# One change to a hybrid decoder layer: the 256-token blocks in plain float32 instead of rounded pairs

## The chip, the cores and the metric

The kernel is one launch on one core of one Trainium2 chip. The metric is the device time of that launch in microseconds. The core has TensorE (PE in the profile, with its weight loads as PEld), VectorE (DVE), ScalarE (ACT), GpSimd (POOL) and SyncE (SP), each with its own queue of instructions that it runs in order, and 16 DMA engines that all the queues share.

## The reference

One decoder layer on 1024 tokens of width 1024, all in float32. The input is normalised and projected; three branches read the projection (a state-space mixer with a short convolution, a gated mixer over positions, and cross-attention to 256 memory tokens), each goes through its own block of `w_branch`, is weighed by a sigmoid gate, and the sum goes through `w_out` and is added to x. Then a mixture of 16384 single-neuron experts is added: 8 heads, each with two sets of 128 keys, the best 16 of each set, the best 16 of their 256 sums. Shortened:

```
proj = rms_norm(x) @ w_in ; z, xbc, dt, u, v, q, gates = split(proj)
merged = sum_n sigmoid(gates_n) * (branch_n @ w_branch_n)      # ssd, gmlp, memory
x = x + merged @ w_out ; xt = rms_norm(x)
sc = (xt @ w_peer_q) . peer_keys ; top 16 per half ; top 16 of the sums -> eid, gate
x = x + sum_k gate_k * gelu(peer_u[eid_k] . xt) * peer_v[eid_k]
return rms_norm(x)
```

## The kernel before

**Tokens.** `BLOCKS` (line 24) are 256, 256 and 512 tokens. A block goes through `mixer` (line 316): 12 convolution tiles (`conv_tile`), the chunk steps of the state-space branch (`chunk_a`, `chunk_b`), z and v, the three branches, the output projection; then `routing` (line 661) chooses its experts. The routing of one block is written beside the convolutions and gates of the next (`beside`, `spill`), and it shares one buffer (`shared`) with the next block's second chunk step. Keys and values of the memory (`mem_norm`, `mem_kv`) are made first.

**Rounded pairs.** Every large product is taken in pairs. A weight tile of 128 x 1024 float32 is loaded by `unit` (line 167) into `raw`, cast by ScalarE to the rounded type float32r (`whi`, line 160), and its rest `wlo` is the difference, taken by GpSimd or, by a share `lo_dve`, by VectorE (line 161). Activations are split in the same way, on ScalarE and VectorE (lines 225, 247, 288, 553, 610, 628). `mm3` (lines 187 to 189) is then three matmuls: hi x hi, hi x lo, lo x hi. `feat` runs 8 such triples on one weight tile with features as output rows (256 or 512 columns, by the block's tokens); `tok` runs 4 weight tiles over all of a block's 128-token tiles with 512 columns. Small products (scores against the keys, attention, line 608, line 579) are plain float32 matmuls already. There are three `raw` buffers and every fourth unit of the mixer uses a fourth one, three `whi` and three `wlo`.

**Experts.** The first 512 tokens (the two blocks of 256) fetch their chosen rows: `gathered` (line 783) issues, for each of 4 tiles of 128 tokens, 128 gathers of u rows and 128 of v rows on GpSimd's queue, 1024 in all; VectorE multiplies each (lines 803 and 810). They are written last in the program. The last 512 tokens run densely over all 16384 experts (`gate_matrix`, `dense_act`, `dense`).

**What sets the order.** A planner places instructions by their position in the program unless `tc.cur_priority` is set, and lets an engine run what is ready. Each `unit` leaves a mark: its priority, its ACT cast (`first`), its subtraction (`second`, or the last one of GpSimd if VectorE took it), and a rate. `pace` (line 1012) picks a mark for a gather: for the first 37 slots (74 gathers) a mark of the second block's units or of the routing beside them, by the rates 0.25 and 0.36; then none up to slot 270; from there a mark of the dense stage. Where there is a mark, the gather takes its priority and `tc.issue_after(m0[2].ins)` (line 792) queues it behind that subtraction on GpSimd.

Of the kernel before, what the change touches and what calls it, by code (L numbers as in the profile page):

```python
# [8 lines left out]
F32 = mybir.dt.float32  # L9
# [49 lines left out]
def layer_kernel(ctx, tc, a, out_d):  # L59
# [104 lines left out]
    lo_dve, share = [0], [0.0]  # L164
    in_mix = [True]

    def unit(src, n=D, k=KD):
        prio = tc.cur_priority
        if in_mix[0] and len(marks) % 4 == 3:
            raw = tmp.tile([P, D], F32, tag="raw4", name="raw", bufs=1)  # L170
        else:
            raw = wts.tile([P, D], F32, tag="raw", name="raw")
        dst = raw[:, :n]
        if len(src.shape) == 3:
            dst = dst.rearrange("p (k c) -> p k c", k=src.shape[1])
        nc.sync.dma_start(dst, src)
        hi = wts.tile([P, D], F32R, tag="whi", name="whi")
        lo = wts.tile([P, D], F32R, tag="wlo", name="wlo")
        share[0] += lo_dve[0]
        on_dve = share[0] >= 1  # L180
        share[0] -= on_dve
        first, second = split(hi[:, :n], lo[:, :n], raw[:, :n], nc.vector if on_dve else nc.gpsimd)
        marks.append((prio, first, marks[-1][2] if on_dve and marks else second, rate[0]))
        return (hi[:, :n].rearrange("p (k c) -> p k c", k=k), lo[:, :n].rearrange("p (k c) -> p k c", k=k))
# [4 lines left out]
        nc.tensor.matmul(ps, lhsT=l_lo, rhs=r_hi, start=False, stop=stop)  # L189

    def feat(src, act, ps=None):
        hi, lo = unit(src)
        if ps is None:
            ps = mm_ps()[:, :act[0].shape[-1]]
        for k in range(KD):
            mm3(ps, hi[:, k, :], lo[:, k, :], act[0][:, k, :], act[1][:, k, :], k == 0, k == KD - 1)
        return ps

    def tok(src, act):
        nt = act[0].shape[-1] // P  # L200
        pss = [mm_ps() for _ in range(nt)]
        for kk in range(4):
            hi, lo = unit(src[kk], k=2)
            for t in range(nt):
                for j in range(2):
                    k = kk * 2 + j
                    s = slice(t * P, (t + 1) * P)
                    mm3(pss[t], act[0][:, k, s], act[1][:, k, s], hi[:, j, :], lo[:, j, :],
                        k == 0, k == KD - 1)
        return pss  # L210

    def act_tiles(n=T):
        if n <= T // 2:
            t = a16(F32R)
            return tuple(t[:, j * KD * n:(j + 1) * KD * n].rearrange("p (k t) -> p k t", k=KD) for j in range(2))
        return (a16(F32R).rearrange("p (k t) -> p k t", k=KD), a16(F32R).rearrange("p (k t) -> p k t", k=KD))

    def transposed(dst, src, t):
        ts = slice(t * P, (t + 1) * P)
        for k4 in range(2):  # L220
            ps = tp_ps()
            for j in range(4):
                k = k4 * 4 + j
                nc.tensor.transpose(ps[:, j * P:(j + 1) * P], src[:, k * P:(k + 1) * P], ident)
            split(dst[0][:, k4 * 4:k4 * 4 + 4, ts], dst[1][:, k4 * 4:k4 * 4 + 4, ts],
                  ps.rearrange("p (j t) -> p j t", j=4))


    def mem_norm():
        m_tok = b16().rearrange("p (t d) -> p t d", t=4)  # L230
        nc.sync.dma_start(m_tok[:, 0:2, :], a["mem"].rearrange("(t p) d -> p t d", p=P))
        ss = sml.tile([P, 2], F32, tag="ssm", name="ss")
        for t in range(2):
            sumsq(col(ss, t), m_tok[:, t, :], m_tok[:, 2 + t, :])
        r = rstd_of(ss, 2)
        for t in range(2):
            nc.vector.tensor_scalar(m_tok[:, t, :], m_tok[:, t, :], col(r, t), None, op0=ALU.mult)
        mT = a16(F32R)
        hi = mT[:, 0:2048].rearrange("p (k m) -> p k m", k=KD)
        lo = mT[:, 2048:4096].rearrange("p (k m) -> p k m", k=KD)  # L240
        for k in range(KD):
            ps = tp_ps()
            for t in range(2):
                nc.tensor.transpose(ps[:, t * P:(t + 1) * P], m_tok[:, t, k * P:(k + 1) * P], ident)
            g = col(pk, PK_LN_MEM + k)
            nc.scalar.activation(hi[:, k, :], ps[:, 0:256], AF.Copy, scale=g)
            nc.vector.scalar_tensor_tensor(lo[:, k, :], ps[:, 0:256], g, hi[:, k, :].bitcast(F32),
                                           op0=ALU.mult, op1=ALU.subtract)
        return hi, lo

    def mem_kv(mT):
        for f in range(8):
# [26 lines left out]
    def x_turn(x_sb, gains):  # L279
        TT = x_sb.shape[1]  # L280
        hT = act_tiles(TT * P)
        for k in range(KD):
            ps = tp_ps()
            for t in range(TT):
                nc.tensor.transpose(ps[:, t * P:(t + 1) * P], x_sb[:, t, k * P:(k + 1) * P], ident)
            g = col(pk, gains + k)
            nc.scalar.activation(hT[0][:, k, :], ps[:, :TT * P], AF.Copy, scale=g)
            nc.vector.scalar_tensor_tensor(hT[1][:, k, :], ps[:, :TT * P], g, hT[0][:, k, :].bitcast(F32),
                                           op0=ALU.mult, op1=ALU.subtract)
        return hT  # L290

    def conv_tile(f, hT, dst, turned):
        T = hT[0].shape[-1]
        ps = feat(a["win_a"][FA_XBC + f], hT)
        cw = PK_CONVW + f * 4
        ac = t2()[:, :T]
        nc.scalar.activation(ac, ps, AF.Identity, bias=col(pk, PK_CONVB + f), scale=col(pk, cw + 3))
        for j in range(3):
            s = 3 - j
            nc.vector.scalar_tensor_tensor(ac[:, s:T], ps[:, 0:T - s], col(pk, cw + j), ac[:, s:T],  # L300
                                           op0=ALU.mult, op1=ALU.add)
            nc.vector.scalar_tensor_tensor(ac[:, 0:s], hist[:, f, j:3], col(pk, cw + j), ac[:, 0:s],
                                           op0=ALU.mult, op1=ALU.add)
        nc.scalar.copy(hist[:, f, :], ps[:, T - 3:T])  # L304
        src = ac if dst is None else dst
        nc.scalar.activation(src, ac, AF.Silu)
        if turned is not None:
            tp = tp_ps()
            for c in range(T // P):
                nc.tensor.transpose(tp[:, c * P:(c + 1) * P], src[:, c * P:(c + 1) * P], ident)  # L310
            nc.scalar.copy(turned, tp[:, :T].rearrange("p (c d) -> p c d", c=T // P))
# [4 lines left out]
    def mixer(b, hT, lmt=None):  # L316
# [20 lines left out]
            nsm[0] += 1  # L337
            return bc[:, o:o + NS].rearrange("p (c h) -> p c h", c=TT)

        hi, lo = unit(a["w_dt"], n=128)  # L340
        fps = mm_ps()[:, :T]
        for k in range(KD):
            mm3(fps[0:16, :], hi[:, k, :], lo[:, k, :], hT[0][:, k, :], hT[1][:, k, :], k == 0, k == KD - 1)
        dtT = tT()
        nc.scalar.copy(dtT[0:16, :], fps[0:16, :])
        conv_tile(4, hT, None, xy[:, :, 4 * P:5 * P])
# [191 lines left out]
        for g in range(8):  # L538
# [11 lines left out]
                                           col(pk, PK_GMLP + g), bs[:, None, :].to_broadcast([P, TT, P]),  # L550
                                           op0=ALU.mult, op1=ALU.add)
            nc.gpsimd.tensor_tensor(m1, m1, ug, op=ALU.mult)
            split(yT[0][:, g, :], yT[1][:, g, :], m1)
        branch(1, yT)


# [47 lines left out]
        def values(h, pTs):  # L604
            for f in range(2):
                op = mm_ps()[:, :T]
                for j in range(2):
                    nc.tensor.matmul(op, lhsT=vm[:, j, h * 256 + f * P:h * 256 + (f + 1) * P], rhs=pTs[j],
                                     start=(j == 0), stop=(j == 1))
                split(yT[0][:, 2 * h + f, :], yT[1][:, 2 * h + f, :], op)  # L610

        prs = attend(0, query(0))
        for h in range(1, H_XA):
# [11 lines left out]

        mT = act_tiles(T)
        for k in range(KD):
            split(mT[0][:, k, :], mT[1][:, k, :], merged[:, k, :])
        ss2 = sml.tile([P, 2, TT], F32, tag="ss2", name="ss2")
        for j in range(2):  # L630
            pss = tok(a["out_b"][j], mT)
# [27 lines left out]


    def routing(xnT, rt, gt=None, eid=None, beside=lambda: None):
        T = xnT[0].shape[-1]
        TT = T // P
        NK = 16 * TT
        U = 16 * NK
# [117 lines left out]
    def gathered(tt, eid, gt, pace):  # L783
        rs = slice(tt * P, (tt + 1) * P)

        def rows_of(table, k, half):
# [2 lines left out]
            if m0:  # L789
                tc.cur_priority = m0[0]  # L790
            g = gat.tile([P, D], F32, tag=f"g4{k % NG}", name="g4", bufs=1)
            with (tc.issue_after(m0[2].ins) if m0 else nullcontext()):
                nc.gpsimd.indirect_dma_start(out=g, out_offset=None, in_=a[table],  # L793
                                             in_offset=bass.IndirectOffsetOnAxis(ap=eid[:, k:k + 1], axis=0))
            if m0:
# [5 lines left out]
        for k in range(SLOTS):  # L801
            g, m1 = rows_of("u", k, 0)
            nc.vector.scalar_tensor_tensor(g, g, 1.0, xn, op0=ALU.mult, op1=ALU.mult, accum_out=col(w, k))  # L803
        with (tc.issue_after(m1[1].ins) if m1 else nullcontext()):
            nc.scalar.activation(w, w, AF.Gelu_apprx_tanh)
        nc.vector.tensor_tensor(w, w, gt, op=ALU.mult)
        acc = held(x2_d[rs, :])
# [134 lines left out]
    for b in range(1, len(BLOCKS)):  # L942
# [12 lines left out]
        def spill(count):  # L955
            for _ in range(count):
                n, f = early.pop(0)
                T = hT[0].shape[-1]
                sgt = t2()[:, :T]
                sigmoid_gate(sgt, hT, n, f)  # L960
                nc.sync.dma_start(gate_d[b][n * KD + f], sgt)
# [9 lines left out]
        lo_dve[0] = 0 if b == 1 else LO_MIXER  # L971
        rate[0] = RATE_MIXER if b == 1 else 0
        now = nxt
        chunks = hT[0].shape[-1] // P
        for _ in range(chunks):
            until(nxt, "chunk")
            spill(KD // chunks)
# [109 lines left out]
```

## Time and profile before

| | |
|---|---|
| time, median of 3 runs | 3783.42 us (3782.95 to 3789.14) |
| profiled execution: time | 3783.22 us |
| profiled execution: span of its instructions | 3781.2 us, clock 0.938 |
| busy: PE, PEld | 3319.3 us (88%), 2794.8 us (74%) |
| busy: DVE, POOL, ACT | 3014.4 us (80%), 2579.4 us (68%), 1472.5 us (39%) |
| HBM | 267 GB/s over the span |

The page gives each engine's busy time, and then the span in 40 equal slices, with the clock that was granted to TensorE in tenths. An average over the span hides that the stages have different limits, so the stretches below matter more. Groups of instructions are named by line, engine, operation and tiles, with their count, busy time and mean. Ends of matmuls are modelled; the distance between two starts is what they really take when they stand back to back.

### The profile page before, as it was taken

The numbers are of one execution on the slowest core, as the hardware profiler recorded it, in microseconds if no ns is written. First come the engines' busy times: TensorE is split into PE (matmuls) and PEld (weight loads), VectorE is DVE, ScalarE is ACT, GpSimd is POOL, SyncE is SP. The second block draws the span as 40 slices with busy tenths as digits, with TensorE's granted clock in tenths as the row PEclk, the third lists the DMA queues.
The fourth block names the chain that finished last, engine by engine and source line by source line (L and its number), as shares of the span: only waits on it lengthen the run. The fifth ranks groups of instructions, "written<-read, shape, count | busy, mean of one in ns | idle before, by whom it ended". The sixth has DMA issues, their size and how long they took to land. (4 is left out here: it accounts for less than half of the span.)

```text
span 3781.2 us, 49410 instructions
## 1 busy us (share of the span) xinstructions
PE 3319.3 (88%) x16928; PEld 2794.8 (74%) x16928; DVE 3014.4 (80%) x5393; ACT 1472.5 (39%) x2239; POOL 2579.4 (68%) x1867
## 2 busy tenths in 40 slices
PE   7899977888877759999989886778999999999998
PEld 6689867778756647777767675666888888888776
DVE  3622489753699999878999998995888888888888
ACT  5454555443434433423332333872222223222222
POOL 6478757688776767688777666664676666666664
PEclk9899988899988879999999997998999999999999
DMA  5255555477787768999998763358999999999997
GB/s 192 69 170 193 185 178 183 158 239 257 278 315 240 240 212 304 345 352 348 339 364 275 250 227 130 156 200 305 342 343 351 328 355 333 339 347 346 332 337 256
DMA packets 353436, 1012.82 MB, mean 268 GB/s; under 512 B 32544, under 2 KB 117920, under 8 KB 350752
## 3 DMA queue, kind: packets, MB, share of 16 engines
q0 software_dynamic: 147456, 536.94, 38.8%
q1 hardware_dynamic: 205728, 472.72, 36.7%
q8 instruction: 134, 2.20, 0.2%
q14 instruction: 118, 0.97, 0.1%
HBM read 945.56 MB, written 63.96 MB: 267 GB/s over the span
## 5 line engine op out<-in xcount | busy, mean ns | idle before, releaser
L161 POOL TENSOR_TENSOR wlo<-raw,whi 128x1024 fp32r<-128x1024 f32 x491 | 1179.3, 2406 | 483.0 <-ACT whi L160 360.8
L160 ACT CAST whi<-raw 128x1024 fp32r<-128x1024 f32 (+1 forms) x623 | 648.1, 1044 | 1163.5 <-issue 364.2
L187 PE MATMUL mm_ps<-a,whi 128*128 128x256 f32 (+2 forms) x2552 | 865.3, 343 | 102.1 <-ACT hist L304 33.8
L189 PE MATMUL mm_ps<-a,wlo 128*128 128x256 f32 (+2 forms) x2552 | 858.3, 339 | 37.7 <-POOL wlo L161 37.4
L188 PE MATMUL mm_ps<-a,whi 128*128 128x256 f32 (+2 forms) x2552 | 860.1, 338 | 3.2 <-DVE a L161 1.9
L793 POOL DMA_INDIRECT g<-in_v_dram,eid x512 | 529.1, 1033 | 304.9 <-DVE row_ps L810 104.7
L803 DVE SCALAR_TENSOR_TENSOR g<-g,row_ps 128x1024 f32<-128x1024 f32 x512 | 606.7, 1211 | 103.9 <-DMA g<-in_u_dram,eid 90.8
L793 POOL DMA_INDIRECT g<-in_u_dram,eid x512 | 529.4, 1034 | 215.4 <-DVE g L803 91.0
L810 DVE SCALAR_TENSOR_TENSOR row_ps<-g,dots,row_ps 128x1024 f32<-128x1024 f32 x512 | 655.7, 1281 | 7.9 <-ACT row_ps L780 1.2
L187 PEld LDWEIGHTS mm_ps<-a,whi 128*128 128x128 f32 (+1 forms) x2552 | 509.0, 201 | 158.4 <-ACT hist L304 36.0
L189 PEld LDWEIGHTS mm_ps<-a,wlo 128*128 128x128 f32 (+1 forms) x2552 | 507.7, 200 | 90.3 <-POOL wlo L161 48.2
L188 PEld LDWEIGHTS mm_ps<-a,whi 128*128 128x128 f32 (+1 forms) x2552 | 511.0, 200 | 47.1 <-DVE a L161 3.4
L188 PE MATMUL mm_ps<-wlo,d 128*128 128x512 f32 x1024 | 406.3, 397 | 0.2 <-POOL wlo L161 0.2
L189 PE MATMUL mm_ps<-whi,d 128*128 128x512 f32 x1024 | 403.5, 396 | 0.0
L187 PE MATMUL mm_ps<-whi,d 128*128 128x512 f32 x1024 | 384.0, 397 | 18.9 <-ACT d L160 16.8
L187 PE MATMUL tp_ps<-a,whi 128*128 128x512 f32 x768 | 302.4, 394 | 10.4 <-ACT d L927 10.4
L189 PE MATMUL tp_ps<-a,wlo 128*128 128x512 f32 x768 | 302.7, 394 | 3.6 <-POOL wlo L161 2.0
L188 PE MATMUL tp_ps<-a,whi 128*128 128x512 f32 x768 | 302.1, 393 | 0.0
L161 DVE TENSOR_TENSOR wlo<-raw,whi 128x1024 fp32r<-128x1024 f32 x132 | 183.8, 1393 | 77.3 <-ACT whi L160 66.3
L187 PEld LDWEIGHTS mm_ps<-whi,d 128*128 128x128 f32 x1024 | 192.9, 188 | 66.7 <-ACT d L160 17.1
L188 PEld LDWEIGHTS mm_ps<-wlo,d 128*128 128x128 f32 x1024 | 193.0, 188 | 47.1 <-POOL wlo L161 0.6
L189 PEld LDWEIGHTS mm_ps<-whi,d 128*128 128x128 f32 x1024 | 193.0, 188 | 46.2
(261 smaller groups left out, 5149.1 us busy)
## 6 DMA issues: line engine op xcount, KB each, us to landing
raw<-in_win_a_dram SPq DMA_DIRECT2D x156, 512.0 KB
raw<-in_uT_a_dram SPq DMA_DIRECT2D x128, 512.0 KB
raw<-in_v_b_dram SPq DMA_DIRECT2D x128, 512.0 KB
raw<-in_br_a_dram SPq DMA_DIRECT2D x72, 512.0 KB
g_d<-a SPq DMA_DIRECT2D x16, 2048.0 KB
a<-g_d SPq DMA_DIRECT2D x32, 1024.0 KB
raw<-in_win_b_dram SPq DMA_DIRECT2D x48, 512.0 KB
raw<-in_pq_a_dram SPq DMA_DIRECT2D x48, 512.0 KB
```

The source lines that it names most:

```text
L160: return (nc.scalar.copy(hi, src), (eng or nc.vector).tensor_tensor(lo, src, hi.bitcast(F32), op=ALU.subtract))
L161: (eng or nc.vector).tensor_tensor(lo, src, hi.bitcast(F32), op=ALU.subtract))
L187: nc.tensor.matmul(ps, lhsT=l_hi, rhs=r_hi, start=start, stop=False)
L188: nc.tensor.matmul(ps, lhsT=l_hi, rhs=r_lo, start=False, stop=False)
L189: nc.tensor.matmul(ps, lhsT=l_lo, rhs=r_hi, start=False, stop=stop)
L793: nc.gpsimd.indirect_dma_start(out=g, out_offset=None, in_=a[table], in_offset=bass.IndirectOffsetOnAxis(ap=eid[:, k:k + 1], axis=0))
L803: nc.vector.scalar_tensor_tensor(g, g, 1.0, xn, op0=ALU.mult, op1=ALU.mult, accum_out=col(w, k))
L810: nc.vector.scalar_tensor_tensor(acc, g, col(w, k), acc, op0=ALU.mult, op1=ALU.add)
```

## The change

Blocks of 256 tokens, the memory and their routing use plain float32 products. `act_tiles` gives one float32 tile instead of a pair where the block has 256 tokens, and each helper asks `plain(act)`: then the weight tile goes from `raw` straight to one matmul per k, nothing is cast or subtracted, and the activation is one copy on ScalarE. `unit(..., whole=True)` leaves a mark without instructions, so the gathers that are paced by such a mark keep its priority and aren't queued behind anything. The 512-token block and the dense stage are as before. Cut to its core (the same test stands in `transposed`, `mem_norm`, `x_turn`, `w_dt`, and where activations are split):

```diff
+    def plain(act):
+        return not isinstance(act, tuple)
-    def unit(src, n=D, k=KD):
+    def unit(src, n=D, k=KD, whole=False):
...
         nc.sync.dma_start(dst, src)
+        if whole:
+            marks.append((prio, None, None, rate[0]))
+            return raw[:, :n].rearrange("p (k c) -> p k c", k=k)
...
     def feat(src, act, ps=None):
+        if plain(act):
+            w = unit(src, whole=True)
+            ps = mm_ps()[:, :act.shape[-1]]
+            for k in range(KD):
+                nc.tensor.matmul(ps, lhsT=w[:, k, :], rhs=act[:, k, :], start=k == 0, stop=k == KD - 1)
+            return ps
...
+    def settle(dst, src):
+        if plain(dst):
+            nc.scalar.copy(dst, src)
+        else:
+            split(dst[0], dst[1], src)
...
     def tok(src, act):
...
+            if plain(act):
+                w = unit(src[kk], k=2, whole=True)
+            else:
+                hi, lo = unit(src[kk], k=2)
...
+                    if plain(act):
+                        nc.tensor.matmul(pss[t], lhsT=act[:, k, s], rhs=w[:, j, :], start=k == 0, stop=k == KD - 1)
+                        continue
...
     def act_tiles(n=T):
         if n <= T // 2:
-            t = a16(F32R)
-            return tuple(t[:, j * KD * n:(j + 1) * KD * n].rearrange("p (k t) -> p k t", k=KD) for j in range(2))
+            return a16()[:, 0:KD * n].rearrange("p (k t) -> p k t", k=KD)
...
-            with (tc.issue_after(m0[2].ins) if m0 else nullcontext()):
+            with (tc.issue_after(m0[2].ins) if m0 and m0[2] else nullcontext()):
```

## Rows read from the trace of the kernel before

**Rows 1.** Stretches: length, busy us (instructions) by engine, clock, DMA share, GB/s

```profile
0.00:476.00 476.00, 418.20 (x2878) 384.65 (x2878) 193.03 (x291) 243.97 (x415) 331.14 (x170) 0.96 0.49 162
476.00:720.00 244.00, 181.69 (x1227) 172.35 (x1228) 209.52 (x722) 138.28 (x225) 160.64 (x110) 0.84 0.51 168
720.00:1040.00 320.00, 276.00 (x1704) 244.11 (x1703) 176.24 (x267) 133.22 (x212) 246.90 (x158) 0.94 0.73 253
1040.00:1350.00 310.00, 235.76 (x1181) 199.38 (x1180) 306.08 (x775) 135.25 (x199) 214.96 (x173) 0.85 0.78 261
1500.00:1945.00 445.00, 412.21 (x1808) 330.24 (x1807) 374.71 (x506) 146.97 (x231) 343.05 (x275) 0.96 0.94 348
1945.00:2330.00 385.00, 330.46 (x1399) 265.73 (x1398) 371.35 (x1144) 119.56 (x159) 267.19 (x192) 0.93 0.71 245
2560.00:3781.00 1221.00, 1191.64 (x5136) 965.68 (x5136) 1031.86 (x1249) 347.21 (x458) 760.31 (x575) 0.99 0.92 331
```

**Rows 2.** Stretches, the gathers of line 793 alone: POOL busy (count)

```profile
476.00:720.00 244.00, 24.08 (x25) 0.84 0.51 168
720.00:1040.00 320.00, 57.27 (x58) 0.94 0.73 253
1500.00:1945.00 445.00, 207.74 (x202) 0.96 0.94 348
1945.00:2330.00 385.00, 101.57 (x105) 0.93 0.71 245
```

**Rows 3.** Timeline of PE, first block's attention: start, length, instruction, count

```profile
357.67 0.28 PE L187 MATMUL mm_ps<-a,whi 128*128 128x256 f32 x1
357.79 0.28 PE L188 MATMUL mm_ps<-a,whi 128*128 128x256 f32 x1
357.91 0.28 PE L189 MATMUL mm_ps<-a,wlo 128*128 128x256 f32 x1
...
361.66 1.89 PE L608 MATMUL mm_ps<-t,b 128*128 128x256 f32 x8
```

**Rows 4.** All of line 608: count, shortest/median/longest ns, starts, forms

```profile
L608 PE MATMUL mm_ps<-t,b x96: 377/379/1219, 361.7 to 1818.7; 128*128 128x256 f32 x64, 128*128 128x512 f32 x32
```

**Rows 5.** Timeline of weight loads in the 512-token block

```profile
1765.33 0.19 PEld L608 LDWEIGHTS mm_ps<-t,b 128*128 128x128 f32 x1 [0.24 <-issue]
1765.76 0.19 PEld L187 LDWEIGHTS mm_ps<-a,whi 128*128 128x128 f32 x1 [0.24 <-ACT t L586]
1766.19 0.19 PEld L188 LDWEIGHTS mm_ps<-a,whi 128*128 128x128 f32 x1 [0.24 <-issue]
1766.42 0.19 PEld L189 LDWEIGHTS mm_ps<-a,wlo 128*128 128x128 f32 x1
```

**Rows 6.** Groups by line and form, 0 to 1040 us: count, busy us, mean ns

```profile
L161 POOL TENSOR_TENSOR wlo<-raw,whi 128x1024 fp32r<-128x1024 f32 x236 | 568.0, 2415 | 213.1 <-ACT whi L160 205.6 <-ACT hist L304 3.8 <-PE tp_ps L596 1.5
L187 PE MATMUL mm_ps<-a,whi 128*128 128x256 f32 x1408 | 416.1, 299 | 49.3 <-ACT hist L304 22.5 <-ACT t L314 13.1 <-ACT b L427 4.7
L160 ACT CAST whi<-raw 128x1024 fp32r<-128x1024 f32 x238 | 248.6, 1046 | 295.5 <-issue 102.9 <-PE mm_ps L188 84.2 <-PE mm_ps L189 50.0
L187 PE MATMUL mm_ps<-whi,a 128*128 128x512 f32 x224 | 81.3, 401 | 2.7 <-ACT whi L160 2.1 <-DVE t L511 0.5
```

**Rows 7.** Timeline, routing of the first block

```profile
570.84 2.38 POOL L161 TENSOR_TENSOR wlo<-raw,whi 128x1024 fp32r<-128x1024 f32 x1
...
571.63 1.62 DVE L302 SCALAR_TENSOR_TENSOR t<-hist,pk,t 128x1 f32<-128x1 f32 x1
```

**Rows 8.** Groups of DVE by line and form, 476 to 720 us

```profile
L705 DVE TENSOR_TENSOR b<-topv 128x48 f32<-128x48 f32 x16 | 14.7, 925 | 0.0
L302 DVE SCALAR_TENSOR_TENSOR t<-hist,pk,t 128x3 f32<-128x3 f32 x10 | 10.8, 1076 | 0.0
```

**Rows 9.** All of line 705 in the 256-token blocks: shortest/median/longest ns

```profile
L705 DVE TENSOR_TENSOR b<-topv x32: 181/195/4077, 502.5 to 1348.5; 128x48 f32<-128x48 f32 x32
```

**Rows 10.** Stretch, the subtractions of line 161 alone: DVE busy, POOL busy

```profile
1040.00:1350.00 310.00, 3.87 (x5) 101.06 (x43) 0.85 0.78 261
```

**Rows 11.** Waits, 476 to 1040 us: total us, times, longest

```profile
DVE t L511 <- DMA t<-gate_d: 13.1, 3, 7.9
```

More of the change, by code (lines that the diff above doesn't have):

```diff
@@ L197, in feat, with tokens_of, part @@
         return ps
+    def tokens_of(act):
+        return (act if plain(act) else act[0]).shape[-1]
+    def part(act, *at):
+        return act[at] if plain(act) else (act[0][at], act[1][at])
+    def settle(dst, src):
[3 more added lines that the diff above has]
+            split(dst[0], dst[1], src)
     def tok(src, act):
-        nt = act[0].shape[-1] // P
+        nt = tokens_of(act) // P
         pss = [mm_ps() for _ in range(nt)]
         for kk in range(4):
-            hi, lo = unit(src[kk], k=2)
+            if plain(act):
+                w = unit(src[kk], k=2, whole=True)
+            else:
+                hi, lo = unit(src[kk], k=2)
             for t in range(nt):
@@ L224, in transposed @@
                 nc.tensor.transpose(ps[:, j * P:(j + 1) * P], src[:, k * P:(k + 1) * P], ident)
-            split(dst[0][:, k4 * 4:k4 * 4 + 4, ts], dst[1][:, k4 * 4:k4 * 4 + 4, ts],
-                  ps.rearrange("p (j t) -> p j t", j=4))
+            settle(part(dst, slice(None), slice(k4 * 4, k4 * 4 + 4), ts), ps.rearrange("p (j t) -> p j t", j=4))
     def mem_norm():
@@ L237, in mem_norm @@
             nc.vector.tensor_scalar(m_tok[:, t, :], m_tok[:, t, :], col(r, t), None, op0=ALU.mult)
-        mT = a16(F32R)
-        hi = mT[:, 0:2048].rearrange("p (k m) -> p k m", k=KD)
-        lo = mT[:, 2048:4096].rearrange("p (k m) -> p k m", k=KD)
+        mT = act_tiles(MEM)
         for k in range(KD):
@@ L245, in mem_norm @@
             g = col(pk, PK_LN_MEM + k)
[L246 to L249, printed above, removed]
+            nc.scalar.activation(mT[:, k, :], ps[:, 0:256], AF.Copy, scale=g)
+        return mT
     def mem_kv(mT):
@@ L286, in x_turn @@
             g = col(pk, gains + k)
-            nc.scalar.activation(hT[0][:, k, :], ps[:, :TT * P], AF.Copy, scale=g)
+            nc.scalar.activation((hT if plain(hT) else hT[0])[:, k, :], ps[:, :TT * P], AF.Copy, scale=g)
+            if plain(hT):
+                continue
             nc.vector.scalar_tensor_tensor(hT[1][:, k, :], ps[:, :TT * P], g, hT[0][:, k, :].bitcast(F32),
@@ L292, in conv_tile @@
     def conv_tile(f, hT, dst, turned):
-        T = hT[0].shape[-1]
+        T = tokens_of(hT)
         ps = feat(a["win_a"][FA_XBC + f], hT)
@@ L338, in s64 @@
             return bc[:, o:o + NS].rearrange("p (c h) -> p c h", c=TT)
-        hi, lo = unit(a["w_dt"], n=128)
+        w_dt = unit(a["w_dt"], n=128, whole=plain(hT))
         fps = mm_ps()[:, :T]
         for k in range(KD):
-            mm3(fps[0:16, :], hi[:, k, :], lo[:, k, :], hT[0][:, k, :], hT[1][:, k, :], k == 0, k == KD - 1)
+            if plain(hT):
+                nc.tensor.matmul(fps[0:16, :], lhsT=w_dt[:, k, :], rhs=hT[:, k, :], start=k == 0, stop=k == KD - 1)
+            else:
+                mm3(fps[0:16, :], w_dt[0][:, k, :], w_dt[1][:, k, :], hT[0][:, k, :], hT[1][:, k, :], k == 0, k == KD - 1)
         dtT = tT()
@@ L552, in mixer @@
             nc.gpsimd.tensor_tensor(m1, m1, ug, op=ALU.mult)
-            split(yT[0][:, g, :], yT[1][:, g, :], m1)
+            settle(part(yT, slice(None), g), m1)
         branch(1, yT)
@@ L609, in values @@
                                      start=(j == 0), stop=(j == 1))
-                split(yT[0][:, 2 * h + f, :], yT[1][:, 2 * h + f, :], op)
+                settle(part(yT, slice(None), 2 * h + f), op)
         prs = attend(0, query(0))
@@ L627, in mixer @@
         for k in range(KD):
-            split(mT[0][:, k, :], mT[1][:, k, :], merged[:, k, :])
+            settle(part(mT, slice(None), k), merged[:, k, :])
         ss2 = sml.tile([P, 2, TT], F32, tag="ss2", name="ss2")
@@ L661, in routing @@
     def routing(xnT, rt, gt=None, eid=None, beside=lambda: None):
-        T = xnT[0].shape[-1]
+        T = tokens_of(xnT)
         TT = T // P
@@ L803, in gathered @@
             nc.vector.scalar_tensor_tensor(g, g, 1.0, xn, op0=ALU.mult, op1=ALU.mult, accum_out=col(w, k))
-        with (tc.issue_after(m1[1].ins) if m1 else nullcontext()):
+        with (tc.issue_after(m1[1].ins) if m1 and m1[1] else nullcontext()):
             nc.scalar.activation(w, w, AF.Gelu_apprx_tanh)
@@ L957, in spill @@
                 n, f = early.pop(0)
-                T = hT[0].shape[-1]
+                T = tokens_of(hT)
                 sgt = t2()[:, :T]
@@ L973, in layer_kernel @@
         now = nxt
-        chunks = hT[0].shape[-1] // P
+        chunks = tokens_of(hT) // P
         for _ in range(chunks):
```

## The prediction

> **What bounds the kernel now.** I read the stretches first. 0 to 476 us (call it M: the memory's keys and values, and the first 256-token block) keeps TensorE (PE) busy 418 of 476 us at a clock of 0.96 [rows 1]: the first limit is PE. 476 to 720 (A: the first block's routing beside the second block's convolutions and gates) has PE at 182 of 244 but VectorE (DVE) at 210 [rows 1]: a chain of small DVE steps, and the chunk step of the second block shares a buffer with the routing, so it can't run past it. 720 to 1040 (B: the rest of the second block) is PE again, 276 of 320, with GpSimd (POOL) at 247. 1040 to 1350 (C: the second block's routing) is DVE at 306 of 310. 1500 to 1945 (the 512-token block) is PE, 412 of 445. 1945 to 2330 (D: the last routing) is DVE, 371 of 385, beside PE at 330. From 2560 on, the dense stage is PE, 1192 of 1221 [rows 1]. The gathers stand across all this: 25 in A, 58 in B, 202 from 1500 to 1945, 105 in D [rows 2]. In A and B they are held to a pace by an order behind POOL's subtraction (line 792); from the 75th to the 540th nothing holds them, and DVE fills with them. The chain of waits reaches back only to the dense stage, so the earlier stretches have to be read one by one.
>
> **PE's price.** In rounded pairs a 256-column product takes three matmuls 0.12 us apart (357.67, 357.79, 357.91) [rows 3], 0.36 us per k. A plain float32 product is not one matmul on this chip: line 608 has 32 statements of 256 columns in the two small blocks (2 blocks, 4 heads, 2 f, 2 j) and 16 of 512 in the large one, and the trace holds 64 and 32 records, two for each statement [rows 4]. Eight such records take 1.89 us from first start to last end, each lasting 0.379 [rows 3, 4], so they start (1.89 - 0.379) / 7 = 0.216 us apart, and a plain product costs 0.432. At 512 columns the weight loads stand 0.43 apart behind a plain record and 0.23 behind a rounded one (1765.33, 1765.76, 1766.19, 1766.42) [rows 5]: 0.86 against 0.69. So a unit of `feat` (8 k) goes from 2.88 to 3.46, +0.58 us, and a unit of `tok` (4 products) from 2.76 to 3.44, +0.7 us. By 1040 us there are 1408 / 8 = 176 units of the first kind and 224 / 4 = 56 of the second [rows 6]; 16 more `feat` units are in C. In all 192 x 0.58 + 56 x 0.7 = 150 us more work for PE. By place in the code: M +73 (88 and 32 units), A +24, B +45 (49 and 24), C +9.
>
> On plain products the trace shows the two records of 0.216 us. The Trainium skill (FP8 and Floating Point Precision, TensorE Precision Notes) says true FP32 makes four passes through the array; a plain record would then be two passes of 0.108, so the row agrees in kind, but the rounded ones here don't reach 0.108, which makes the ratio 1.2 and not 4/3. A price by the page's ratio is the last rival below.
>
> **What is removed.** Each unit loses a ScalarE (ACT) cast of 1.05 us (238 by 1040) and a POOL subtraction of 2.4 us (236 by then) [rows 6]; the activations lose their DVE subtraction. POOL's time is worth more than its own: while it subtracts, small DVE steps wait. A 128x1 step, line 302, begins at 571.63 and lasts 1.62 us while POOL subtracts from 570.84 for 2.38 [rows 7]; line 705's 128x48 add has a minimum of 181 ns and a mean of 925 in A [rows 8, 9]: 16 x 0.74 = 12 us. Line 302's 32 steps there, of which the 10 of 128x3 have a mean of 1076 [rows 8], give 20 us in the same way, and four smaller groups (lines 428, 730, 738, 702) some 15: 47 us of A's 210, in six groups of which two stand. All of POOL's subtractions in A go, and 16 of the 43 in C [rows 10]; the rest of C's belong to the 512-token block and stay. So C gets about 16/43 of a like sum back, some 20 us.
>
> **What moves.** (1) The order that held the first 74 gathers hangs on the subtraction, and is gone with it; only their priority is left. POOL and DVE are free enough to run them early. In B, the rate of the stretch where nothing holds them, 202 in 445 us [rows 2], gives 150 in 335 us where 58 stand now; DMA engines at 0.94 there against 0.73 in B [rows 1] are why I count on 60 to 90 more, not on all. In A, DVE would be at 163 without the waits; up to 220 us there is room for (220 - 163) / 1.28 = 45 more, 1.28 us each (line 803, 1.20 us and its accumulator read). Together 105 to 135 more by the end of B. The 540 free ones then run out before D instead of inside it. Each early gather also stands 1.0 us in POOL's queue (24.08 / 25 [rows 2]) ahead of the routing's multiply of line 741, where a subtraction of 2.4 us stood. (2) A raw weight buffer is given back by PE's last matmul, not by POOL. Line 176's load waits for PE now, and behind it on SyncE stand the gate stores and the routing's key loads, whose readers are ScalarE's buffers and PE. Four units are left where seven were in line before (four raw, three split); three ahead are 10.4 us of PE work, and the longest wait for a load in A and B is 7.9 us (gate_d, three waits, 13.1 in all) [rows 11]. I count nothing for it under that cover; if it is gone, some 13 us as those waits, and not below nothing, since no load comes earlier.
>
> **The sum**, on the profiled execution (span 3781.2, 3783.2 with what lies around it; the median of the runs is 3783.4).
> - M: PE-bound, +73, less about 16 of PE's 58 idle us, which wait for subtractions, casts and the DVE step after a transpose: +57. Bounds +40 (most idle time gone) to +73.
> - A: 244 to 220: DVE 210 - 47, filled up by early gathers; PE at 182 + 24 = 206 allows it: -24. Bounds: -38 (PE's 206) and +36 (DVE 163 and all 112 gathers that seven heads make ready, (112 - 25) x 1.28 = 111, together 274 and 280 with gaps).
> - B: +45 of PE against 44 idle us: +15. Nearest row: 1500 to 1945 idles 7% under free gathers; B would be (276 + 45) x 1.04. Bounds -15 (waits of B's DVE steps gone too) and +45.
> - C: -20. Bounds -40 and 0 (gathers fill the gap).
> - 1350 to 1945: nothing; the same pairs, the same gathers.
> - D: DVE's 371 hold 105 x 1.28 = 134 us of gathers. Without them PE ends last, at 330 of 385: -55 at most; -45 with some ten gathers left. Bound 0 (none came forward).
> - Dense stage: nothing; its gathers are paced from 540 on, whenever the earlier ones ended.
> Sum: 57 - 24 + 15 - 20 - 45 = -17, so **3766 us**.
>
> **The rivals.**
> 1. *My case*: PE's price is paid in M and half of B, and earned back by DVE in A, C and D. 3766, own range 3725 to 3790. Chance 0.48.
> 2. *Slower: the freed gathers fill the routing.* Place: DVE's queue in A. Each is 1.28 us that can't be interrupted in a chain of steps of 0.2 to 0.3 us. It decides once more than about 88 run in A, (244 - 163) / 1.28 + 25. For it: C, where nothing holds them, is 310 us long for the same 256 tokens, with DVE full. Against it: C also carries 512-wide convolutions, and heads release their 16 slots one after another. M +60, A +36, B +25, C 0, D -50: +71, 3854. Chance 0.24.
> 3. *Gathers stay where they are*, by their priority. A -40 (nothing fills it), B +5, C -20, D 0, M +55: 0, 3783. Against it: from the 75th on they run with the lowest priority of all, and still 202 go in 445 us. Chance 0.13.
> 4. *Faster: waits behind POOL were most of the idle time.* M +45, A -38, B -10, C -40, D -55: -98, 3685. For it: A's PE clock of 0.84 and C's 0.85 [rows 1] could rise with fewer pauses. Chance 0.12.
> 5. *Four passes at the rounded rate*: 4 x 0.12 = 0.48 per k and 4 x 0.23 = 0.92 at 512 columns, 192 x 0.96 + 56 x 0.92 = 236 us instead of 150; M +92, B +70 instead of +57 and +15: +73, 3856. Line 608's rows speak against it. Chance 0.03. This is the 4/3 that the page of the Trainium skill named above would give.
>
> **How the numbers follow.** Likeliest: 3766. Cases 2 and 5 lie above, 4 below; leaving out the upper half of 2 and the lower half of 4 gives 3690 to 3850, which also holds the bounds of A and D. About 0.2% (7.6 us) is what a measurement can tell from no change. Faster by more: three quarters of case 1 and all of 4 and a little of 3, 0.57. Same: the middle of 3 and a slice of 1, 0.13. Slower: 2, 5 and the ends of 1 and 3, 0.30.
>
> **What would show it.** Line 608's pitch on `feat`: 16 records of 0.216 per unit; M ending near 533; A some 24 us shorter with about 70 gathers, line 705 near 0.2 us; over 180 gathers before block three's convolutions; none left in D, which ends with PE. Wrong if A grows (case 2), if D keeps a hundred gathers (case 3), or if PE waits for raw weights (the 10.4 us of cover are too little).

## The result, and the profile after

The changed kernel takes 3828.6 us (median of 4 runs, 3824.1 to 3834.3), the kernel before 3786.0 in the same comparison: a ratio of 1.0116, 95% interval 1.0101 to 1.0132. It is slower; the forecast was 3766 and faster. The profiled execution took 3834.3 us.

The stretches of after, cut where the same work stands as in [rows 1] (length, then busy us and instructions of PE, weight loads, DVE, ACT and POOL, then clock, DMA share, GB/s):

```profile
0.00:520.00 520.00, 486.90 (x2038) 371.87 (x2038) 93.86 (x237) 126.51 (x291) 35.44 (x47) 0.97 0.49 150
520.00:785.00 265.00, 201.47 (x911) 170.11 (x912) 216.89 (x819) 95.41 (x185) 109.77 (x121) 0.86 0.75 261
785.00:1112.00 327.00, 301.21 (x1229) 221.77 (x1228) 87.09 (x174) 64.03 (x137) 48.01 (x55) 0.98 0.57 186
1112.00:1395.00 283.00, 234.88 (x1034) 188.37 (x1035) 272.23 (x758) 118.77 (x183) 177.34 (x159) 0.92 0.85 292
1540.00:1985.00 445.00, 412.45 (x1797) 330.66 (x1796) 378.04 (x508) 150.20 (x234) 338.94 (x271) 0.95 0.94 345
1985.00:2375.00 390.00, 328.46 (x1392) 262.93 (x1391) 359.95 (x1123) 118.89 (x157) 250.03 (x175) 0.93 0.65 219
2608.00:3832.00 1224.00, 1193.04 (x5136) 965.73 (x5136) 1033.96 (x1249) 347.61 (x458) 756.97 (x575) 0.99 0.93 330
```

M is 44 us longer than in [rows 1] and has become nearly pure PE (487 of 520). A is 21 longer, though PE and DVE have less than 265 to do. In B both DVE and POOL stand nearly empty (87 and 48 of 327), which was the room that the forecast filled with gathers. C is 27 shorter, D 5 longer.

The gathers alone (line 824 of after, line 793 before; the answer to [rows 2]):

```profile
520.00:785.00 265.00, 76.79 (x80) 0.86 0.75 261
785.00:1112.00 327.00, 19.40 (x21) 0.98 0.57 186
1540.00:1985.00 445.00, 202.61 (x198) 0.95 0.94 345
1985.00:2375.00 390.00, 86.31 (x89) 0.93 0.65 219
```

A took 80 where 25 stood, B only 21 where 58 stood, and D still has 89. Why they stop is in the timeline of POOL (start, length, engine, line; the idle time before and its releaser in brackets). These are the last early gather, the last routing step behind it, and what comes at 1063:

```profile
769.70 0.93 POOL L824 DMA_INDIRECT g<-in_u_dram,eid  x1 [0.60 <-DVE g L834]
770.93 0.94 POOL L824 DMA_INDIRECT g<-in_u_dram,eid  x1 [0.30 <-DVE bp L748]
775.55 1.10 POOL L772 TENSOR_TENSOR b<-b,topi 128x512 bf16<-128x512 bf16 x1 [0.42 <-DVE b L769]
...
1063.29 2.34 POOL L161 TENSOR_TENSOR wlo<-raw,whi 128x1024 fp32r<-128x1024 f32 x1 [20.89 <-ACT whi L160]
1065.78 0.98 POOL L824 DMA_INDIRECT g<-in_u_dram,eid  x1
1066.83 2.39 POOL L161 TENSOR_TENSOR wlo<-raw,whi 128x1024 fp32r<-128x1024 f32 x1
```

Between 771 and 1066 us no gather is issued, and POOL has some 20 us of work. The gather at 1065.78 waited for the subtraction just ahead of it. In the code, 117 marks serve the 74 early gathers, and not all of them come from the second block and the routing beside it, as the account of `pace` ahead of the prediction has it: 113 belong to those plain units, which leave no subtraction, but the last four are convolutions of the 512-token block, which are still split. The 74th gather (slot 36.5) takes the first of those. 80 gathers are out by 771: the 73 ahead of it and the next seven, which no order holds. Then the eight buffers of `rows_of` are full: the 82nd needs the buffer of the 74th, and that one stands behind a unit 290 us away. That this hold alone keeps the later gathers back is tested by `e1_free74` below.

What the new instructions cost PE, from its timeline in M (`feat`, 48 records of 256 columns; `tok`, 24 of 512):

```profile
44.15 10.53 PE L203 MATMUL mm_ps<-a,raw 128*128 128x256 f32 x48
64.92 10.46 PE L238 MATMUL mm_ps<-raw,a 128*128 128x512 f32 x24
```

Less the length of one record (0.38 and 0.59), the distance between two starts is (10.53 - 0.38) / 47 = 0.216 us and (10.46 - 0.59) / 23 = 0.429: the pitches that [rows 3 to 5] gave.

### The profile page after: what moved, and what is told of

Same layout as the page of the kernel before. It is cut to its first block, busy times and chain, and to the rows that moved or that the text cites. A ratio compares the mean times of both kernels' runs of the same rounds, so it can differ in the third digit from the quotient of the medians.

```text
span 3832.3 us, 44924 instructions
## 1 busy us (share of the span) xinstructions
PE 3433.6 (90%) x15152; PEld 2745.2 (72%) x15152; DVE 2787.4 (73%) x5297; ACT 1231.7 (32%) x1989; POOL 1971.8 (51%) x1617
## 4 chain that ended last, share of the span: by engine, by line
PE 33%; DVE 14%; issue 4%; DMA 2%; POOL 2%; ACT 2%; DVEq 0%; SPq 0%; ACTq 0%; POOLq 0%
PE mm_ps L194 7%; PE mm_ps L195 7%; PE mm_ps L196 7%; PE tp_ps L196 4%; PE tp_ps L195 4%; PE tp_ps L194 4%; DVE d L858 2%; DVE row_ps L841 2%; DVE d L860 1%; DVE g L834 1%; POOL g L824 1%; ACT a L872 1%; DMA raw<-in_v_b_dram 1%; POOL wlo L161 1%; DVE a L733 1%
## 5 line engine op out<-in xcount | busy, mean ns | idle before, releaser
L203 PE MATMUL mm_ps<-a,raw 128*128 128x256 f32 x3072 | 708.2, 389 | 48.9 <-ACT b L458 26.3
L161 POOL TENSOR_TENSOR wlo<-raw,whi 128x1024 fp32r<-128x1024 f32 (+1 forms) x241 | 580.4, 2409 | 286.7 <-ACT whi L160 171.8
L203 PEld LDWEIGHTS mm_ps<-a,raw 128*128 128x128 f32 x3072 | 593.9, 196 | 138.4 <-ACT b L458 26.5
L160 ACT CAST whi<-raw 128x1024 fp32r<-128x1024 f32 x373 | 388.4, 1048 | 834.1 <-PE mm_ps L196 248.6
L196 PE MATMUL mm_ps<-a,wlo 128*128 128x512 f32 (+1 forms) x1000 | 406.4, 407 | 53.3 <-POOL wlo L161 53.0
L194 PE MATMUL mm_ps<-a,whi 128*128 128x512 f32 (+1 forms) x1000 | 404.0, 410 | 14.7 <-ACT b L458 7.3
L195 PE MATMUL mm_ps<-a,whi 128*128 128x512 f32 (+1 forms) x1000 | 404.9, 405 | 0.9 <-DVE a L161 0.9
L196 PEld LDWEIGHTS mm_ps<-a,wlo 128*128 128x128 f32 (+1 forms) x1000 | 194.8, 195 | 109.8 <-POOL wlo L161 68.4
L194 PEld LDWEIGHTS mm_ps<-whi,d 128*128 128x128 f32 x1024 | 193.0, 189 | 72.6 <-ACT d L160 20.3
L194 PEld LDWEIGHTS mm_ps<-a,whi 128*128 128x128 f32 (+1 forms) x1000 | 195.0, 195 | 60.2 <-ACT b L458 7.6
```

The costliest lines, as they stand in the source:

```text
L160: return (nc.scalar.copy(hi, src), (eng or nc.vector).tensor_tensor(lo, src, hi.bitcast(F32), op=ALU.subtract))
L161: (eng or nc.vector).tensor_tensor(lo, src, hi.bitcast(F32), op=ALU.subtract))
L194: nc.tensor.matmul(ps, lhsT=l_hi, rhs=r_hi, start=start, stop=False)
L195: nc.tensor.matmul(ps, lhsT=l_hi, rhs=r_lo, start=False, stop=False)
L203: nc.tensor.matmul(ps, lhsT=w[:, k, :], rhs=act[:, k, :], start=k == 0, stop=k == KD - 1)
```

## The experiments

Ratios are to the kernel before, from runs beside it. To compare the kernels stage by stage, one profiled execution of each is cut at events of the program: PE's first transpose of the first block's routing input (end of M), the start of the second block's second chunk step (end of A), the second block's routing input (end of B), the third block's second chunk step (end of C), the scores of the last routing (end of the large block), the gate matrix (end of D). These cuts lie up to 45 us beside those of [rows 1], and the sum of a kernel's stages moves up to 8 us from its median.

```
us                M    A    B    C  large   D  rest | gathers in A    B  large   D
before          483  239  343  330   549  388  1449 |             25   70   249 105
after           526  259  342  306   549  394  1456 |             80   28   245  90
e1_free74       522  259  394  300   522  312  1455 |             90  195   153   9
e2_held         524  216  360  309   551  396  1455 |             25   76   247  97
e3_pe_alone     549  261  380  331   548  397  1452 |             25   71   246 104
e4_relief       450  195  314  299   549  385  1456 |             27   76   246  99
e5_pace_a       522  239  406  313   529  313  1454 |             63  201   169   9
e6_first_paired 479  244  406  316   525  314  1453 |             63  200   170   9
e7_before_free  483  312  423  336   532  312  1452 |             87  176   174   9
e8_routing_plain 478 221  347  310   542  383  1452 |             24   73   246 100
```

**PE's price without the relief of ScalarE and GpSimd.** `e3_pe_alone` keeps the plain products, but the casts and GpSimd's subtractions run as before, into tiles that nothing reads. Two things don't come back with them: the DVE subtractions of the activations, and PE's own waits for cast and subtracted weights.

```
         if whole:
-            marks.append((prio, None, None, rate[0]))
+            hi = wts.tile([P, D], F32R, tag="whi", name="whi")
+            lo = wts.tile([P, D], F32R, tag="wlo", name="wlo")
+            first, second = split(hi[:, :n], lo[:, :n], raw[:, :n], nc.gpsimd)
+            marks.append((prio, first, second, rate[0]))
```

> The changed kernel, but each plain unit still runs its cast on ScalarE and its subtraction on GpSimd into tiles that nothing reads, so that TensorE's longer products are alone, without the relief of the other engines, and the gathers keep their old pace. Theory 3 (the relief of GpSimd and VectorE is worth some 50 to 80 us and pays for part of TensorE's price): 3870 to 3910, with the first stretch at 525 to 545 us, the first routing at 245 to 265 and the second block's later part at 345 to 365. Rival (the relief is worth nothing; the price is all that is seen): within 15 us of the kernel with the pace put back.

Measured: 3917.8 us, 1.0346 of before (1.0325 to 1.0367), +130: M +66, A +22, B +37, C +1, D +9. Kernel, M and B lie a little above the expected ranges. The stretch M of the kernel before, then of `e3_pe_alone`:

```profile
0.00:483.00 483.00, 420.28 (x2885) 385.54 (x2885) 199.34 (x306) 248.88 (x428) 333.50 (x171) 0.96 0.50 164
0.00:549.00 549.00, 493.90 (x2045) 373.91 (x2046) 145.32 (x250) 248.85 (x428) 325.65 (x171) 0.96 0.46 143
```

At the same mean clock PE is busy 74 us longer in M, and DVE 54 us less. PE's busy time grows by 18 in A, 42 in B and 10 in C in the same way: 144 in all.

**The old pace with nothing to subtract.** `e2_held` is after, but each plain unit leaves a mark again, a subtraction of one column on GpSimd, so the gathers come as before:

```
         if whole:
-            marks.append((prio, None, None, rate[0]))
+            tick = sml.tile([P, 1], F32, tag="tick", name="tick")
+            held_by = nc.gpsimd.tensor_tensor(tick, raw[:, 0:1], raw[:, 0:1], op=ALU.subtract)
+            marks.append((prio, None, held_by, rate[0]))
```

> The changed kernel with the old pace put back: each plain unit runs one 128x1 subtraction on GpSimd, and its mark names it, so the early gathers are queued behind it as they were behind the 2.4 us one. Theory 2 (the first block's routing became longer, 244 to 265 us, because 80 gathers instead of 25 fill VectorE's queue there): about 25 gathers in that stretch, which takes 205 to 230 us; the next stretch takes on some 60 gathers and is 0 to 15 us longer; the kernel is at 3785 to 3805. Rival (the stretch is longer because TensorE has 24 us more work there, with waits): it stays at 260 to 270 us with 25 gathers, and the kernel at 3825 to 3840.

Measured: 3809.5 us, 1.0056 (1.0037 to 1.0076), +22: M +41, A -23, B +17, C -21, D +8. A is as expected; the kernel lies a little above its range and below the rival's. Against `e3_pe_alone`, which differs by the casts and subtractions alone, it is 108 us faster: M -25, A -45, B -20, C -22. The stretch A of `e3_pe_alone`, then of `e2_held`:

```profile
549.00:810.00 261.00, 199.69 (x899) 166.86 (x900) 207.91 (x706) 129.64 (x214) 161.65 (x111) 0.89 0.48 152
524.00:740.00 216.00, 189.15 (x900) 160.33 (x899) 160.02 (x709) 87.62 (x170) 67.75 (x109) 0.95 0.57 185
```

DVE's busy time falls by 48, as A does by 45. Where from stands in DVE's groups by line and form there (count, busy us, mean ns of one), the first two lines of `e3_pe_alone`, the last two of `e2_held`:

```profile
L739 DVE TENSOR_TENSOR b<-topv 128x48 f32<-128x48 f32 x16 | 19.4, 1216 | 0.0
L333 DVE SCALAR_TENSOR_TENSOR t<-hist,pk,t 128x3 f32<-128x3 f32 x8 | 3.6, 448 | 0.0
```

```profile
L738 DVE TENSOR_TENSOR b<-topv 128x48 f32<-128x48 f32 x16 | 3.2, 199 | 0.0
L332 DVE SCALAR_TENSOR_TENSOR t<-hist,pk,t 128x3 f32<-128x3 f32 x8 | 1.7, 218 | 0.0
```

The first of each pair is line 705 of [rows 8], the second line 302: the same steps on the same data, on average 6 and 2 times as long in the kernel in which GpSimd subtracts. These two groups are 18 of the 48 us; with the 128x1 form of line 332 and three more two-input steps (lines 762, 766 and 783 of `e2_held`) it is some 42. The Trainium skill (SBUF — State Buffer, Who interferes with whom) says that a DVE instruction with two inputs in SBUF contends with a GpSimd instruction that reads SBUF; these rows agree. How long such a step waits is seen in [rows 7]: it ends at 573.25 us, and the subtraction at 573.22.

**GpSimd's subtraction alone.** `e4_relief` is the kernel before without the subtraction of the weights of the memory and the two small blocks; their `lo` is replaced by `hi`, so that part of the result is left out. PE's work is that of before:

```
+        if small:
+            first = nc.scalar.copy(hi[:, :n], raw[:, :n])
+            tick = sml.tile([P, 1], F32, tag="tick", name="tick")
+            held_by = nc.gpsimd.tensor_tensor(tick, raw[:, 0:1], raw[:, 0:1], op=ALU.subtract)
+            marks.append((prio, first, held_by, rate[0]))
+            h = hi[:, :n].rearrange("p (k c) -> p k c", k=k)
+            return h, h
```

> The kernel before, in rounded pairs with its three matmuls, but in the memory's and the two small blocks' units the subtraction of the weights is left out (a 128x1 subtraction on GpSimd stands for it in the pace, and the third matmul takes the cast weights again, so the rest of the weights is missing from the result). It shows the relief of GpSimd alone, with TensorE's work as before. Theory 3: the waits of VectorE's small steps behind GpSimd go; the first routing shrinks from 244 to 205 to 225 us, the second from 310 to 280 to 295, the first stretch by 10 to 20; kernel at 3700 to 3735. Rival (those waits are hidden beside TensorE or filled by gathers): within 15 us of 3786.

Measured: 3646.6 us, 0.9629 (0.9609 to 0.9648), -141: M -33, A -44, B -29, C -31. This is below the expected 3700 to 3735: the relief is worth more than was thought. The casts are still there, so the A -44 is the subtraction's. Work that never stands on PE costs 3.7% of the kernel, through the waits that it makes; in the kernel before, up to 1395 us, PE's matmuls waited for it only 14 us and its weight loads 21.

**The hold on the 74th gather.** `e1_free74` is after without any order ahead of the dense stage; the only orders left there were those of the four units of the large block:

```
-            with (tc.issue_after(m0[2].ins) if m0 and m0[2] else nullcontext()):
+            with (tc.issue_after(m0[2].ins) if m0 and m0[2] and n >= NPRE else nullcontext()):
```

> The changed kernel with no gather held behind a subtraction before the dense stage (line 823 asks for n >= NPRE as well). In the changed kernel 73 row products run up to 769 us, then none until 1073: the 74th gather is paced by a mark of the 512-token block, which still has a subtraction, and the ring of eight buffers stops behind it. Theory 1 (this one hold keeps the gathers out of the second block's later part, and so in the last routing): 90 to 150 gathers between 785 and 1112 instead of 21, few or none in the last routing (89 there now), which becomes 30 to 50 us shorter; whole kernel 3780 to 3800. Rival (the last routing is bound by its own VectorE chain or by TensorE, whatever the gathers do): the gathers move but the last routing stays at 380 to 390 us, and the kernel stays within 10 us of 3829.

Measured: 3763.6 us, 0.9934 (0.9914 to 0.9953): 65 us under after, and more than was expected (D fell by 82 and not by 30 to 50). Stretches of A, B and D, and the gathers in them:

```profile
522.00:781.00 259.00, 194.62 (x899) 164.29 (x899) 219.32 (x816) 85.72 (x160) 116.63 (x129) 0.88 0.77 273
781.00:1175.00 394.00, 319.82 (x1248) 230.60 (x1248) 312.96 (x423) 78.83 (x168) 215.43 (x231) 0.91 1.01 398
1997.00:2309.00 312.00, 304.31 (x1407) 253.30 (x1406) 231.23 (x1008) 118.69 (x155) 176.39 (x97) 0.99 0.44 133
```

```profile
522.00:781.00 259.00, 85.81 (x90) 0.88 0.77 273
781.00:1175.00 394.00, 184.26 (x195) 0.91 1.01 398
1997.00:2309.00 312.00, 8.70 (x9) 0.99 0.44 133
```

B takes 195 gathers, with the DMA engines busy all the time (share 1.01); D has 9 left and is PE at 304 of 312 at a clock of 0.99. Half of what D gained stands in PE's waits, first of after, then of `e1_free74` (us in total, times, longest):

```profile
PE mm_ps L196 <- POOL wlo L161: 36.5, 21, 5.3
PE tp_ps L196 <- POOL wlo L161: 5.6, 2, 5.3
```

```profile
PE mm_ps L196 <- POOL wlo L161: 0.3, 1, 0.3
```

With 90 gathers in D, PE waits 42 us for subtractions; with 9, 0.3. The wait doesn't go by the number of gathers alone: in the kernel before it is 28 us with 105.

**Fewer gathers in A.** `e5_pace_a` keeps the tick of `e2_held` where the rate is that of the routing, and holds early gathers only there:

```
+            held_by = None
+            if rate[0] == RATE_ROUTING:
+                tick = sml.tile([P, 1], F32, tag="tick", name="tick")
+                held_by = nc.gpsimd.tensor_tensor(tick, raw[:, 0:1], raw[:, 0:1], op=ALU.subtract)
+            marks.append((prio, None, held_by, rate[0]))
...
-            with (tc.issue_after(m0[2].ins) if m0 and m0[2] else nullcontext()):
+            with (tc.issue_after(m0[2].ins) if m0 and m0[2] and (n >= NPRE or m0[3] == RATE_ROUTING) else nullcontext()):
```

> The changed kernel with the old pace (a 128x1 subtraction on GpSimd that stands for the 2.4 us one) in the units beside the first routing alone, and no hold from there to the dense stage. Theory (the hold is worth having where VectorE's routing chain is the limit, and harmful where TensorE is): the first routing takes 205 to 225 us as with the pace everywhere (208), the gathers run on in the second block's later part, the last routing takes 310 to 335 us as with no hold (312); kernel 3715 to 3750. Rival (the gathers that don't run in the first routing only move to later stages, one for one): 3755 to 3775.

Measured: 3773.3 us, 0.9960 (0.9947 to 0.9973). A gets 63 gathers instead of 90 and is 20 us shorter than in `e1_free74`; B, C and the large block give it all back (+12, +13, +7). The rival's range was right: what leaves A comes back later. But B's +12 comes with only 6 gathers more and C's +13 with 3, and both stay unexplained.

**Where plain products pay.** `e6_first_paired` is `e5_pace_a` with rounded pairs again in the memory and the first block's mixer; the second block and both small routings stay plain:

```
-    def act_tiles(n=T):
+    def act_tiles(n=T, pair=False):
+        if n <= T // 2 and pair:
+            t = a16(F32R)
+            return tuple(t[:, j * KD * n:(j + 1) * KD * n].rearrange("p (k t) -> p k t", k=KD) for j in range(2))
...
-        mT = act_tiles(MEM)
+        mT = act_tiles(MEM, True)
...
-        yT = act_tiles(T)
+        yT = act_tiles(T, b == 0)
```

> The same as the run with the pace in the first routing alone, but the memory and the first block's mixer stay in rounded pairs; plain are the second block's units and both small routings. In the memory and the first block the change cost 43 us (483 to 526 up to the first block's last transposes). Theory (that stretch is TensorE's; the price is paid there and nothing later depends on it): the stretch is back at 480 to 490, the rest unchanged, kernel 30 to 45 us under that run. Rival (the first block's subtractions come back on GpSimd and delay the first routing): less than 15 us under it.

Measured: 3736.6 us, 0.9868 (0.9847 to 0.9889), 37 us under `e5_pace_a`, as expected: M -43, A +5, the rest within 4.

`e8_routing_plain` goes the other way: the kernel before, with plain products only in the query projection of the two small routings (16 units each); its marks take the last subtraction, so the pace is the old one. The edit is shown against after:

```
         if whole:
-            marks.append((prio, None, None, rate[0]))
+            marks.append((prio, None, marks[-1][2], rate[0]))
...
-        yT = act_tiles(T)
+        yT = act_tiles(T, True)
```

> The kernel before with plain products in the two small routings alone (32 units of the query projection); all else in rounded pairs; a gather paced by such a unit is queued behind the subtraction before it. Theory (plain products pay where VectorE's chain is the limit: 32 x 0.58 = 18 us of TensorE in stages where it has room, 32 subtractions of 2.4 us less beside VectorE's small steps): the first routing 238 to 215 to 228 us, the second's stage 348 to 325 to 340, kernel 3745 to 3765. Rival (half the subtractions in those stages are left, and they alone hold up the chain): within 12 us of 3787.

Measured: 3737.5 us, 0.9876 (0.9851 to 0.9901): A -18, C -20, nothing lost in M and B; the kernel is faster than the expected 3745 to 3765. `e6_first_paired` and this one beat both kernels; their intervals don't tell them apart.

**The hold in the kernel before.** `e7_before_free` is the kernel before with its early gathers released:

```
-            with (tc.issue_after(m0[2].ins) if m0 else nullcontext()):
+            with (tc.issue_after(m0[2].ins) if m0 and n >= NPRE else nullcontext()):
```

> The kernel before, rounded pairs throughout, with no gather held behind a subtraction ahead of the dense stage. It tells how much of the gain of taking the hold away (3829 to 3764 in the changed kernel) belongs to the hold and not to the plain products. Theory (the hold alone costs it: gathers can run beside the pairs too, though GpSimd is busier): 3740 to 3775, with the last routing shorter by 30 to 70 us than its 388 and the first one longer by 20 to 60. Rival (without the plain products GpSimd and VectorE have no room in the second block, the gathers stay late): 3780 to 3800.

Measured: 3853.0 us, 1.0180 (1.0163 to 1.0197). Both expectations were wrong: the same edit that gains 65 us in after costs 66 here. Its A and B:

```profile
483.00:795.00 312.00, 193.98 (x1262) 183.03 (x1261) 284.44 (x830) 129.23 (x209) 216.09 (x171) 0.79 0.69 232
795.00:1218.00 423.00, 306.10 (x1698) 262.55 (x1699) 328.94 (x396) 142.59 (x228) 365.40 (x279) 0.86 0.94 340
```

POOL at 365 of 423 and DVE at 329 in B carry gathers and subtractions together. What a gather costs goes by the stage it stands in; from the table (stages that differ in more than gathers make this an estimate): after against `e2_held`: A 43 us for 55 gathers, 0.78 each (`e5_pace_a` against `e2_held`: 23 for 38, 0.61). `e1_free74` against after: B 52 us for 167, 0.31; large block 27 for 92, 0.29; D 82 for 81, 1.0. `e7_before_free` against before: A 73 for 62, 1.18; B 80 for 106, 0.75; large block 17 for 75, 0.23; D 76 for 96, 0.79. Moving gathers from D to B paid only where B's subtractions were gone.

## Why the prediction was wrong, step by step

**The step that failed: what moves (1).** "The order that held the first 74 gathers hangs on the subtraction, and is gone with it." It is gone for 73; the 74th kept it, because the marks reach four units into the large block, and behind it the ring of eight buffers and the order of the products stop all others until 1066 us. D, forecast -45, came out at +6, with 90 gathers instead of some ten. `e1_free74`, which makes the sentence true, takes 65 us off. That its 3763.6 lies by the forecast's 3766 is luck; its terms are others: M +39, A +20, B +51, C -30, large block -27, D -76.

**The price of a gather in A and B** was the second error. A, forecast -24 with 70 gathers, came out at +20 with 80, and it is +20 in `e1_free74` too, so this miss doesn't come from the hold. The case and the second rival let A fill for nothing until DVE was full, up to 220 us or up to 88 gathers. With 25 gathers A was 216 us with DVE at 160 (`e2_held`), and 55 more made it 259 with DVE at 213. A was back at its old 239 with 63 gathers (`e5_pace_a`), with DVE at 189: no room was free of charge. That DVE's idle time there lies in a chain of short steps, and can't be filled for that reason, fits these numbers but isn't shown. Whether a gather delays that chain more by its 1 us on POOL or by its 1.28 on DVE, no run here separates. B, forecast +15 with 60 to 90 more gathers, came out at -1 with 42 fewer; with 125 more (`e1_free74`) it is +51, beyond its bound of +45. B's factor of 1.04 has no row behind it: the stretch named beside it, with 412 of 445 us busy, gives 1.08, and +27.

**What held.** Without the moves the forecast's own terms are M +57, A -38 (its bound by PE), B +15, C -20: +14. `e2_held` measures them: +41, -23, +17, -21, also +14; M's and A's errors of some 15 cancel. Another 8 us stand in D and 8 in the large block and the rest of its profiled execution (+30 in all; the medians give +22). Taken singly:
- PE's price: 150 forecast (M 73, A 24, B 45, C 9); PE's busy time grew by 144 in `e3_pe_alone` (74, 18, 42, 10), and the stretches by 66, 22, 37 and 1. The pitches of [rows 3 to 5] held; C hid its part. The last rival's 236 and its +92 in M are not borne out; it also took B's +70 whole, where the case let idle time hide two thirds of +45. It went by the ratio 4/3 that follows from the four passes of the Trainium skill (FP8 and Floating Point Precision, TensorE Precision Notes); the trace doesn't agree with that ratio here, with 0.432 against 0.36 at 256 columns.
- Relief: 47 us of DVE forecast for A; DVE's busy time went from 208 to 160 between `e3_pe_alone` and `e2_held`, and A by 45. C 20 and 22. M was under-sized: 16 forecast, 25 measured.
- Weight loads, what moves (2): counted at nothing, and PE waited 6.2 us in 2 waits for them up to 1110 us. Where gathers fill the DMA engines the cover fails: 18.3 us in B of `e1_free74`.

```profile
PE mm_ps L203 <- DMA raw<-in_br_a_dram: 6.2, 2, 3.9
```

```profile
PE mm_ps L203 <- DMA raw<-in_br_a_dram: 18.3, 3, 16.8
```

- D's bound of -55, "PE ends last, at 330 of 385", was too tight: `e1_free74` gains 76. PE's 332 busy us there ran at a mean granted clock of 0.93; in `e1_free74` it is 0.99, and D's matmuls take 304.

**The rivals.** The second had the right sign and the right place in A (+36 against +20), though A grew before DVE was full, and not its -50 in D; the third, that gathers stay where they are, was right for D and wrong for A. The result is one half of each, a case that the forecast did not have. The signs of what would prove it wrong were named: A grew, and D kept 90 of its hundred gathers. Of the chances one sum is wrong: three quarters of case 1, all of 4 and a little of 3 make about 0.5 and not 0.57.

## What to carry to other kernels

When an edit removes the instruction that other work is ordered behind, list every mark that the ordered work can pick, to the last one: a single one left, behind a ring of buffers, stops all that follows. Price movable work by the stage it leaves and the stage it enters (here 0.8 to 1.0 us in D, 0.3 in B, 0.6 to 0.8 in A), after the edit and not before it. Trade a cheaper engine's preparation for a dearer matmul only where that engine's work delays the chain: here in the routing, not in a stretch that PE already fills.

## What the runs showed of the hardware

Some 250 GpSimd subtractions of 2.4 us, for which PE's matmuls waited only 14 us and its weight loads 21, cost 141 us in all; in A they did so by stretching DVE steps of 0.2 us to 1.2. The granted clock gave something back where pauses went: in D its mean rose from 0.93 to 0.99 of the upper level (2.4 GHz) when PE no longer waited for subtractions. By an estimate from these rows, 332 x 0.93 / 0.99 = 312, some 20 of the 28 us that PE's busy time lost there go with the clock.
